# Output projection and gate as seven block products with 512 columns, weight sums formed by adding transfers

## Chip, cores and metric

One core of one Trainium2 chip. The metric is the device time of one execution in microseconds. TensorE multiplies, VectorE and ScalarE work element by element, GpSimd and SyncE (SP) have queues of their own, and 16 DMA engines move data for every queue.

## What is computed

One layer of a hybrid trunk on 1024 tokens of width 1024, in float32, and a final norm:

```python
u = rms_norm(h, norm_w)
proj = u @ w_in                       # 1024 x 6668, split into the mixers' inputs
o_hg = group_rms_norm(hgrn2_mixer(q, f_logit, i_in, lb), hg_norm_w, 6) * silu(g_hg)
o_pool = pool_mixer(u_pool, pool_w, pool_scale) * silu(g_pool)
y_ssd = ssd_mixer(xbc, dt_raw, ...) * silu(z)
o_ssd = group_rms_norm(y_ssd, ssd_norm_w, 4)
mixed = concatenate([o_hg, o_pool, o_ssd])       # 1024 x 2048
h = h + mixed @ w_out                            # output projection
gate = sigmoid(h @ w_pg)
h = h + gate * (p_i @ w_pe)                      # p_i: 1024 x 256
return rms_norm(h, final_norm_w)
```

## The kernel before

Every float32 product is made of three matmuls on rounded operands: a number is split into `hi` (a cast by ScalarE) and `lo` (the remainder, a subtraction by VectorE), and `mm3` (L163) issues hi x hi, hi x lo and lo x hi. Weights come by `wload` (L130, 512 KB on SP's queue, two buffers `raw`) and are split by `wsplit` (L135, four buffers). `bank` (L96) hands out eight PSUM banks by tags (`mx`, `pj`, `sc`).

The stages in order: the x norm with its transposes into `uh`/`ul` (the tokens transposed, hi and lo) and the v tiles; pool mixing and the gates of the hg part, both already by seven products of two by two blocks (`st_cm`, L327, and `st_tm`, L361, whose sums of weights VectorE makes in `st_cm_w`, L307, and `add`, L371); six hg heads; four SSD groups (L827); the g tiles (L894); the output projection (L927); the gate (L979) and the final norm.

The output projection runs over two halves of the 2048 mixed columns (`ab`) and four pieces of 256 output columns (`q`). For each it makes eight token tiles by `tm_tile` (L182): 8 blocks of 128 x 3 matmuls of 256 columns. `he` adds the bank into `H`, at first together with x (`xr`, 128 KB loads). The operands are put into `uh`/`ul` by `fill` (L846): 96 transposes, a ScalarE and a VectorE op for each bank of four. The y part is multiplied by silu(z) (`z_gate`, L880) and normalised (`y_norm`, L919) between the tiles of `q` = 1. `h_back` (L863) transposes `H` back into `uh`/`ul`. The gate takes four pieces of 256 columns x eight tiles x (24 + 6 for p @ w_pe), then sigmoid, product, sum, square, scaling (L990 to L1002), and in the last piece the root on GpSimd (L1005), the last scaling and the store of 512 KB.

A scheduler orders each engine's instructions by priorities: `high_priority` moves an instruction ahead, `issue_after` holds one back. Each engine and each queue then works in that order, so whatever waits holds all that stands behind it on the same engine.

## Time and profile before

| | us |
|---|---|
| median of 3 runs (1051.61 to 1053.7) | 1052.12 |
| the profiled execution | 1054.85 |
| its span in the trace | 1053.0 |
| TensorE busy in the span | 1027.2 |
| VectorE busy | 620.3 |
| ScalarE busy | 447.9 |
| GpSimd busy | 39.9 |

The span is the time from the first to the last recorded event of the profiled execution; 1.85 us lie around it. Matmuls overlap in the array, so that the sum of their durations is more than the time that they take; where TensorE is busy without a gap, the distance of two starts is the price of one.

### The profile page before, as it was taken

Reading aid. Unit: us, or ns where it says so; the run is one execution under the profiler, and the core shown is the slowest. Engines: PE = TensorE matmul, PEld = TensorE weight load, DVE = VectorE, ACT = ScalarE, POOL = GpSimd, SP = SyncE. Lnnn points to the kernel's source line nnn. Section 1 sums busy time; section 2 is a strip of 40 time slices with the busy share of each in tenths; the row PEclk is TensorE's granted clock in tenths of the full one; section 3 lists DMA queues with packets and bytes.
Section 4 is the critical chain, followed back from the end, with each engine's and each line's share of the span. In section 5 each row is a group of like instructions: output and inputs, shape, how many; then the busy total and the mean of one; then the engine's idle time right before and its main releaser. Section 6 shows DMA issues by size and latency. Waiting matters only on the chain.

```text
span 1053.0 us, 19902 instructions
## 1 busy us (share of the span) xinstructions
PE 1027.2 (98%) x8364; PEld 923.7 (88%) x8364; DVE 620.3 (59%) x1156; ACT 447.9 (43%) x904; POOL 39.9 (4%) x69
## 2 busy tenths in 40 slices
...
GB/s 293 128 66 63 40 100 119 83 61 200 163 22 41 41 22 21 52 41 21 59 72 57 85 40 81 121 139 96 93 118 87 50 141 41 41 41 41 2 21 141
DMA packets 41434, 82.73 MB, mean 79 GB/s; under 512 B 4000, under 2 KB 26880, under 8 KB 41088
## 3 DMA queue, kind: packets, MB, share of 16 engines
...
q14 instruction: 25, 0.20, 0.1%
...
## 4 chain that ended last, share of the span: by engine, by line
PE 81%; DVE 11%; ACT 3%; DMA 3%; issue 1%; POOL 0%; SPq 0%; POOLq 0%; ACTq 0%; DVEq 0%
PE b_pj L166 19%; PE b_pj L165 19%; PE b_pj L167 19%; DVE ar L582 5%; PE b_mx L165 3%; PE b_mx L167 3%; PE b_mx L166 3%; PE b_mx L806 1%; DVE lo L140 1%; PE b_sc L704 1%; PE b_mx L699 1%; PE b_mx L701 1%; DVE blk L601 1%; PE b_sc L167 1%; PE b_sc L166 1%; PE b_sc L165 1%
## 5 line engine op out<-in xcount | busy, mean ns | idle before, releaser
L165 PE MATMUL b_pj<-hi,uh 128*128 128x256 f32 (+1 forms) x1088 | 309.9, 285 | 0.4 <-ACT uh L216 0.4
L166 PE MATMUL b_pj<-lo,uh 128*128 128x256 f32 (+1 forms) x1088 | 307.3, 282 | 0.4 <-DVE lo L140 0.4
L167 PE MATMUL b_pj<-hi,ul 128*128 128x256 f32 (+1 forms) x1088 | 306.6, 282 | 0.2 <-DVE ul L217 0.2
L166 PEld LDWEIGHTS b_pj<-lo,uh 128*128 128x128 f32 x1088 | 205.8, 189 | 1.1 <-DVE lo L140 0.9
L165 PEld LDWEIGHTS b_pj<-hi,uh 128*128 128x128 f32 x1088 | 205.7, 189 | 0.8 <-ACT uh L216 0.6
L167 PEld LDWEIGHTS b_pj<-hi,ul 128*128 128x128 f32 x1088 | 205.5, 189 | 0.4 <-DVE ul L217 0.4
L166 PE MATMUL b_pj<-ul,hi 128*128 128x512 f32 x416 | 168.8, 406 | 0.0
L165 PE MATMUL b_pj<-uh,hi 128*128 128x512 f32 x416 | 168.3, 404 | 0.0
L167 PE MATMUL b_pj<-uh,lo 128*128 128x512 f32 x416 | 167.8, 403 | 0.0
L139 ACT CAST hi<-raw 128x1024 fp32r<-128x1024 f32 (+1 forms) x72 | 73.9, 1026 | 175.6 <-PE b_pj L167 99.0
L140 DVE TENSOR_TENSOR lo<-raw,hi 128x1024 fp32r<-128x1024 f32 (+1 forms) x72 | 85.9, 1194 | 103.5 <-ACT hi L139 91.7
L582 DVE TENSOR_TENSOR ar<-ar 128x512 f32<-128x512 f32 (+8 forms) x168 | 93.9, 594 | 6.5 <-PE b_sc L673 5.0
L166 PEld LDWEIGHTS b_pj<-ul,hi 128*128 128x128 f32 x416 | 78.2, 188 | 17.7
L165 PEld LDWEIGHTS b_pj<-uh,hi 128*128 128x128 f32 x416 | 78.2, 188 | 16.9
L167 PEld LDWEIGHTS b_pj<-uh,lo 128*128 128x128 f32 x416 | 78.2, 188 | 16.7
L748 DVE SCALAR_TENSOR_TENSOR ar<-ar,pr 128x1021 f32<-128x1021 f32 (+2 forms) x42 | 53.7, 1279 | 0.6
L954 DVE TENSOR_TENSOR big<-xr,b_pj 128x256 f32<-128x256 f32 x32 | 13.4, 419 | 50.6 <-PE b_pj L167 50.6
L782 ACT ACTIVATE E<-E,sm 128x128 f32<-128x128 f32 x96 | 32.0, 392 | 25.3 <-DMA E<-cumd 21.0
L956 DVE TENSOR_TENSOR big<-big,b_pj 128x256 f32<-128x256 f32 x32 | 13.4, 419 | 43.5 <-PE b_pj L167 43.5
L1001 ACT ACTIVATE junk<-sg 128x256 f32<-128x256 f32 x32 | 13.4, 418 | 40.2 <-DVE sg L999 40.2
L140 DVE TENSOR_TENSOR lo<-big,hi 128x1024 fp32r<-128x1024 f32 x18 | 21.9, 1222 | 14.0 <-ACT hi L139 14.0
L739 ACT COPY ar<-b_pj 128x512 f32<-128x512 f32 x28 | 16.2, 580 | 31.9 <-PE b_pj L167 31.8
...
## 6 DMA issues: line engine op xcount, KB each, us to landing
raw<-wcm SPq DMA_DIRECT2D x34, 512.0 KB, 3.2
raw<-wo SPq DMA_DIRECT2D x16, 512.0 KB, 3.8
raw<-wtm SPq DMA_DIRECT2D x12, 512.0 KB, 3.2
...
x<-x SPq DMA_DIRECT2D x8, 512.0 KB, 9.4
...
raw<-wg SPq DMA_DIRECT2D x8, 512.0 KB, 3.4
```

The lines of the kernel that those rows point to most:

```text
L139: A.copy(hi[:, :width], raw[:, :width])
L140: V.tensor_tensor(out=lo[:, :width], in0=raw[:, :width], in1=hi[:, :width].bitcast(F32), op=ALU.subtract)
L165: T.matmul(out=o, lhsT=sh, rhs=mh, start=first, stop=False, skip_group_check=more)
L166: T.matmul(out=o, lhsT=sh, rhs=ml, start=False, stop=False, skip_group_check=more)
L167: T.matmul(out=o, lhsT=sl, rhs=mh, start=False, stop=last, skip_group_check=more)
L582: mul = lambda o, x, y: V.tensor_tensor(out=o, in0=x, in1=y, op=ALU.mult)
L739: A.copy(xp[:, c], b)
L748: V.scalar_tensor_tensor(out=y[:, d:], in0=xp[:, : S - d], scalar=cw(i), in1=y[:, d:], op0=ALU.mult, op1=ALU.add)
L782: A.activation(E[:, i, :], E[:, i, :], AF.Relu, scale=-1.0, bias=cum[:, r0 + i : r0 + i + 1])
L954: V.tensor_tensor(out=H[:, t, qc], in0=xr, in1=b, op=ALU.add)
L956: V.tensor_tensor(out=H[:, t, qc], in0=H[:, t, qc], in1=b, op=ALU.add)
L1001: A.activation(junk, sg, AF.Square, accum_out=ssf[:, q, t : t + 1])
```

## The change

- **The products.** The output projection and the gate are each computed as seven products of two by two blocks (`Seven`). A block of tokens is 512 tokens, a block of columns 512 columns; the inner dimension is halved too, into 4 groups of 256 for the projection and 2 for the gate. All matmuls have 512 columns. A product adds into four banks, and banks are read into `H`, or into `Q` for the gate, with signs. Sums of tokens are made by VectorE (`tokens`), sums of weights lie ready in DRAM.
- **Sums of weights.** `sums_by_dma` forms the four sums that a set of weights needs by eight transfers from DRAM to DRAM, four of which add to what lies there. There are eight sets: four for `st_cm` (`tcd`, 256 KB each transfer), two for `st_tm` (`ttd`, 512 KB), one for the projection (`tod`, 2 MB), one for the gate (`tgd`, 1 MB). All 64 are issued by GpSimd's queue after the last root of the x norm. VectorE's sums in `st_cm_w` and `st_tm` are gone, some signs change.
- **Operands through DRAM.** `fill` still transposes; ScalarE copies the bank out and GpSimd's queue stores it (`mtd`). When the last tile is stored, 20 loads on GpSimd's queue bring the operands into `Q` (8 MB, in the space of `uh`/`ul` and others), and 8 more bring x into `H`. The products split tokens group by group (`asplit`). `h_back` puts `H` back into `Q` by ScalarE alone.
- **p @ w_pe** is computed apart, in 16 tiles of 512 columns: 8 ahead of the first product, 8 within the gate; ScalarE's queue stores them (`ped`) and SP loads them for the gate.
- **The y part** is multiplied and normalised by `y_fin` at the end of each SSD group.
- **The gate's end** works on tiles of 128 x 512 (`gate`, `close`); for the second 512 tokens an adding transfer puts the product into `H`.

The diff, without the renamed layouts of weights on the host:

```diff
+    PAIRS_C = ((26, 27), (30, 31), (28, 29), (32, 33))
+    PAIRS_T = ((5, 6), (7, 2))
+    tcd = [dp.tile([P, 2048], F32, name=f"tcd{i}") for i in range(4)]
+    ttd = [dp.tile([P, 4096], F32, name=f"ttd{i}") for i in range(2)]
+    tod = dp.tile([4, 4 * P, 1024], F32, name="tod")
+    tgd = dp.tile([4, 2 * P, 1024], F32, name="tgd")
+    def sums_by_dma(d, b11, b12, b21, b22):
+        t1, t3, t2, t4 = d
+        add = lambda o, i: nc.gpsimd.dma_start(out=o, in_=i, accum_op=ALU.add, max_dma_last_dim=8192)
+        nc.gpsimd.dma_start(out=t3, in_=b22)
+        nc.gpsimd.dma_start(out=t1, in_=b11)
+        add(t3, b12)
+        add(t1, b12)
+        nc.gpsimd.dma_start(out=t2, in_=t3)
+        add(t2, b11)
+        nc.gpsimd.dma_start(out=t4, in_=t2)
+        add(t4, b21)
...
+    with tc.issue_after(rooted.ins):
+        for d, (j0, j1) in zip(tcd, PAIRS_C):
+            sums_by_dma([d[:, i * 512 : i * 512 + 512] for i in range(4)], wcm[j0][:, :512], wcm[j1][:, :512], wcm[j0][:, 512:], wcm[j1][:, 512:])
+        for d, (s0, s1) in zip(ttd, PAIRS_T):
+            sums_by_dma([d[:, i * 1024 : i * 1024 + 1024] for i in range(4)], wtm[2 * s0], wtm[2 * s1], wtm[2 * s0 + 1], wtm[2 * s1 + 1])
+        sums_by_dma([tod[i] for i in range(4)], *(wo[i, j] for i in range(2) for j in range(2)))
...
-    def st_cm_w(j0, j1):
...
-            V.tensor_tensor(out=t1, in0=b12, in1=b11, op=ALU.subtract)
-            V.tensor_tensor(out=t3, in0=b22, in1=b12, op=ALU.subtract)
...
+    def st_cm_w(i):
+        j0, j1 = PAIRS_C[i]
+        w0 = wsplit(wload(wcm[j0], 1024), 1024)
+        w1 = wsplit(wload(tcd[i][:, :1024], 1024), 1024)
+        w2 = wsplit(wload(tcd[i][:, 1024:], 1024), 1024)
+        w3 = wsplit(wload(wcm[j1][:, 512:], 512), 512)
...
+    def st_tm(i, fin):
+        s0, s1 = PAIRS_T[i]
+        srcs = {1: wtm[2 * s0], 2: wtm[2 * s0 + 1], 3: wtm[2 * s1 + 1]}
+        for n, z in enumerate((5, 7, 6, 4)):
+            srcs[z] = ttd[i][:, n * 1024 : n * 1024 + 1024]
...
-        G.memset(a, 0.0)
+        V.memset(a, 0.0)
...
+    def y_fin(g, half):
+        ts, gs = slice(4 * half, 4 * half + 4), slice(g * DG, (g + 1) * DG)
+        sg, sgh = ar.take(768)
+        sg = sg.rearrange("p (c n) -> p c n", n=DG)
+        nc.sync.dma_start(sg, gzd[:, ts, gs])
+        V.tensor_tensor(out=Y[:, ts, gs], in0=Y[:, ts, gs], in1=sg, op=ALU.mult)
+        ar.give(sgh)
+        for t in range(4 * half, 4 * half + 4):
+            junk = sp.tile([P, 256], F32, tag="junk", bufs=1, name="junk")
+            A.activation(junk[:, :DG], Y[:, t, gs], AF.Square, accum_out=ssy[:, g, t : t + 1])
+        rstd(rsy[:, g, ts], ssy[:, g, ts], DG)
+        V.tensor_tensor(out=Y[:, ts, gs], in0=Y[:, ts, gs], in1=rsy[:, g, ts].unsqueeze(2).broadcast_to([P, 4, DG]), op=ALU.mult)
...
+        for half in range(2):
+            y_fin(g, half)
...
+    def fill(src, wcol, ab, half, k):
+        b = bank("mx")
+        for i in range(4):
+            T.transpose(out=b[:, i * P : (i + 1) * P], in_=src[:, half * 4 + i, k * P : (k + 1) * P], identity=ident)
+        z, zh = ar.take(512)
+        with tc.high_priority(offset=EPRIO):
+            A.activation(z, b, AF.Copy, scale=pr[:, wcol + k : wcol + k + 1])
+        nc.gpsimd.dma_start(mtd[half][ab][:, k, :], z)
...
-            for t in range(NT):
-                tm_tile("o", q, 256, t, he, pcs)
-                if q == 0 and t < 3:
-                    fill_step(*((O, P_HW, 0), (Y, P_SW, 2))[ab], 1, t)
-                if ab == 0 and q == 3 and 4 <= t < 7:
-                    fill_step(Y, P_SW, 2, 0, t - 4)
-                if ab == 0 and q == 1:
-                    z_gate(t)
-                    y_norm(t)
...
+    def pe_tile(sg, aw, ew, half, j, t, engine):
+        (ah, al), (eh, el) = aw, ew
+        b = bank("pj")
+        for k in range(2):
+            c, w = slice(k * 512 + t * P, k * 512 + t * P + P), slice(k * 512, k * 512 + 512)
+            mm3(b, ah[:, c], al[:, c], eh[:, w], el[:, w], k == 0, k == 1)
+        with tc.high_priority(offset=EPRIO):
+            engine(sg, b)
+        nc.scalar.dma_start(ped[:, 4 * half + t, HALF[j]], sg)
...
+    for j in range(2):
+        for t in range(4):
+            pe_tile(xw[t][:, :512], pw[0], pw[1 + j], 1, j, t, V.tensor_copy)
...
+    Q = [[fp.tile([P, KD, 512], F32, name=f"q{i}{j}") for j in range(2)] for i in range(2)]
+    for i in range(2):
+        for j in range(2):
+            for g in range(3):
+                nc.gpsimd.dma_start(Q[i][j][:, 2 * g : 2 * g + 2, :], mtd[i][j][:, 2 * g : 2 * g + 2, :])
+            for k in range(2):
+                last = nc.gpsimd.dma_start(Q[i][j][:, 6 + k, :], pod[2 * j + k][:, HALF[i]])
+    with tc.issue_after(last.ins):
+        for t in range(NT):
+            nc.gpsimd.dma_start(H[:, t, :], x[t * P : (t + 1) * P, :])
...
+    def asplit(src):
+        hi = fp.tile([P, 2, 512], F32R, tag="ah", bufs=4, name="ah")
+        lo = fp.tile([P, 2, 512], F32R, tag="al", bufs=4, name="al")
+        with tc.high_priority(offset=WPRIO):
+            A.copy(hi, src)
+            V.tensor_tensor(out=lo, in0=src, in1=hi.bitcast(F32), op=ALU.subtract)
+        return hi, lo
...
+    class Seven:
+        def __init__(self, q, n, w, td):
+            self.q, self.n, self.w = q, n, {1: w[0, 0], 2: w[1, 0], 3: w[1, 1], 5: td[0], 7: td[1], 6: td[2], 4: td[3]}
+        def tokens(self, i, g):
+            a11, a12, a21, a22 = (self.q(r, c, g) for r in range(2) for c in range(2))
+            s2 = S2[:, g]
+            with tc.high_priority(offset=WPRIO):
+                if i == 6:
+                    V.tensor_tensor(out=a21, in0=a11, in1=a21, op=ALU.subtract)
+                    V.scalar_tensor_tensor(out=s2, in0=a22, scalar=-1.0, in1=a21, op0=ALU.mult, op1=ALU.subtract)
+                elif i == 5:
+                    V.scalar_tensor_tensor(out=a11, in0=s2, scalar=-1.0, in1=a11, op0=ALU.mult, op1=ALU.subtract)
+                elif i == 3:
+                    V.scalar_tensor_tensor(out=a12, in0=s2, scalar=-1.0, in1=a12, op0=ALU.mult, op1=ALU.subtract)
+            return asplit({1: a11, 2: a12, 3: a12, 4: a22, 5: a11, 6: s2, 7: a21}[i])
+        def load(self, i, g):
+            return wload(self.w[i][g * P : (g + 1) * P, :], 1024)
+        def mult(self, bs, i, first, evac, by_tile=False):
+            gs = []
+            for g in range(self.n):
+                raw = self.load(i, g)
+                gs.append((self.tokens(i, g), wsplit(raw, 1024)))
+                if not by_tile:
+                    self.part(bs, gs, g, range(4), first)
+            for t in range(4):
+                if by_tile:
+                    for g in range(self.n):
+                        self.part(bs, gs, g, (t,), first)
+                evac(t, bs[t])
+        def part(self, bs, gs, g, ts, first):
+            (ah, al), (bh, bl) = gs[g]
+            for k in range(2):
+                w = slice(k * 512, k * 512 + 512)
+                for t in ts:
+                    c = slice(t * P, (t + 1) * P)
+                    mm3(bs[t], ah[:, k, c], al[:, k, c], bh[:, w], bl[:, w], first and g == 0 and k == 0, g == self.n - 1 and k == 1, not first)
...
+    def onto(i, j, op):
+        def f(t, b):
+            h = H[:, 4 * i + t, HALF[j]]
+            with tc.high_priority(offset=EPRIO):
+                V.tensor_tensor(out=h, in0=h, in1=b, op=op)
+        return f
+    sev = Seven(lambda r, c, g: Q[r][c][:, 2 * g : 2 * g + 2, :], 4, wo, tod)
+    X = four("mx", "mx", "mx", "mx")
+    sev.mult(X, 1, True, onto(0, 0, ALU.add))
+    sev.mult(four("pj", "pj", "sc", "sc"), 2, True, onto(0, 0, ALU.add))
+    sev.mult(X, 6, False, onto(0, 1, ALU.subtract))
+    sev.mult(X, 7, False, onto(1, 1, ALU.subtract))
+    sev.mult(X, 4, False, onto(1, 0, ALU.add))
+    Yb = four("pj", "pj", "sc", "sc")
+    sev.mult(Yb, 5, True, onto(1, 1, ALU.subtract))
+    for t in range(4, 8):
+        h_back(t, 0, "mx")
+    for t in range(4):
+        h_back(t, 0, "mx")
+    for t in range(4, 8):
+        h_back(t, 1, "mx")
+    sev.mult(Yb, 3, False, onto(0, 1, ALU.subtract))
...
+    def gate(i, j, t, src):
+        sg, tt = gq(i, j, t), 4 * i + t
+        h = H[:, tt, HALF[j]]
+        r = rsf[:, tt : tt + 1]
+        pe = fp.tile([P, 512], F32, tag="pe", bufs=3, name="pe")
+        nc.sync.dma_start(pe, ped[:, tt, HALF[j]])
+        with tc.high_priority(offset=EPRIO):
+            A.activation(sg, src, AF.Sigmoid)
+        with tc.high_priority(offset=300):
+            V.tensor_tensor(out=sg, in0=sg, in1=pe, op=ALU.mult)
+            if i == 0:
+                V.tensor_tensor(out=h, in0=h, in1=sg, op=ALU.add)
+            else:
+                nc.gpsimd.dma_start(out=h, in_=sg, accum_op=ALU.add)
+            A.activation(sg, h, AF.Square, accum_out=ssf[:, j, tt : tt + 1])
+            if j == 0:
+                V.tensor_scalar(out=r, in0=ssf[:, 0, tt : tt + 1], scalar1=1.0 / D, scalar2=EPS, op0=ALU.mult, op1=ALU.add)
+                V.tensor_tensor(out=h, in0=h, in1=fwb[:, HALF[0]], op=ALU.mult)
+            else:
+                G.tensor_scalar(out=r, in0=ssf[:, 1, tt : tt + 1], scalar1=1.0 / D, scalar2=r, op0=ALU.mult, op1=ALU.add)
+                G.tensor_tensor(out=r, in0=r, in1=negh[:, :1], op=ALU.pow)
+                V.scalar_tensor_tensor(out=h, in0=h, scalar=r, in1=fwb[:, HALF[1]], op0=ALU.mult, op1=ALU.mult)
+                h0 = H[:, tt, HALF[0]]
+                A.activation(h0, h0, AF.Copy, scale=r)
+        if j == 1:
+            nc.sync.dma_start(out[tt * P : (tt + 1) * P, :], H[:, tt, :])
...
+    sev = Seven(lambda r, c, g: Q[r][0][:, 4 * c + 2 * g : 4 * c + 2 * g + 2, :], 2, wg, tgd)
+    X = four("mx", "mx", "mx", "mx")
+    pw = [pe_part(pT, 0), pe_part(we, 0)]
+    sev.mult(X, 1, True, keep(0, 0, 1.0))
+    for t in range(4):
+        pe_tile(fp.tile([P, 512], F32, tag="pst", bufs=4, name="pst"), *pw, 0, 0, t, A.copy)
+    pw[1] = pe_part(we, 1)
+    sev.mult(X, 6, False, keep(0, 1, -1.0))
+    for t in range(4):
+        h_back(t, 1, "sc")
+    for t in range(4):
+        pe_tile(fp.tile([P, 512], F32, tag="pst", bufs=4, name="pst"), *pw, 0, 1, t, A.copy)
+    sev.mult(X, 7, False, keep(1, 1, -1.0))
+    sev.mult(X, 4, False, lambda t, b: gate(1, 0, t, b))
+    Yb = four("pj", "pj", "sc", "sc")
+    sev.mult(Yb, 5, True, close(1, 1, ALU.subtract))
+    sev.mult(four("mx", "mx", "mx", "mx"), 2, True, close(0, 0, ALU.add), True)
+    sev.mult(Yb, 3, False, close(0, 1, ALU.subtract), True)
```

Three places in the order of instructions. First SP's queue where the weights of the first `st_cm` are loaded, between stores of v tiles (`vd`); before:

```order
L132 DMA raw<-wcm 128x1024
L229 DMA vd<-vs 128x256
L132 DMA raw<-wcm 128x1024
L229 DMA vd<-vs 128x256 x9
L132 DMA raw<-wcm 128x1024
L229 DMA vd<-vs 128x256 x6
L132 DMA raw<-wcm 128x1024
```

and after (`tcd_97` is the first set of sums, 256 KB x 8):

```order
L155 DMA raw<-wcm 128x1024
L253 DMA vd<-vs 128x256
L155 DMA raw<-tcd_97 128x1024
L253 DMA vd<-vs 128x256 x8
L155 DMA raw<-tcd_97 128x1024
L155 DMA raw<-wcm 128x512
L253 DMA vd<-vs 128x256 x7
```

In the place of the second load of raw weights stands a load of the first half of the sums, and in that of the third one of their second half; behind each stand stores of v tiles.

Second ScalarE's queue between the last fill and the first product of the output projection; before (L219 is a fill, L139 the cast of a weight, L216 that of a pool part):

```order
L219 ACTIVATE uh<-b_mx,pr 128x512 x2
L922 ACTIVATE junk,ssy<-ar 128x192
L139 CAST hi<-raw 128x1024
L216 CAST uh<-ar 128x512
L900 ACTIVATE sg<-b_pj 128x256
L216 CAST uh<-ar 128x512
L139 CAST hi<-raw 128x1024
L219 ACTIVATE uh<-b_mx,pr 128x512 x6
L139 CAST hi<-raw 128x1024 x6
L216 CAST uh<-ar 128x512 x2
```

and after (L868 is a fill, L162 the cast of a weight, L926 the store of a p @ w_pe tile, L959 the cast of tokens):

```order
L162 CAST hi<-raw 128x1024
L868 ACTIVATE ar<-b_mx,pr 128x512 x3
L926 DMA ped<-big 128x512 x2
L926 DMA ped<-xw_4848 128x512
L162 CAST hi<-raw 128x1024
L926 DMA ped<-xw_4849 128x512
L926 DMA ped<-big 128x512 x2
L926 DMA ped<-xw_4848 128x512
L162 CAST hi<-raw 128x1024 x2
L926 DMA ped<-xw_4849 128x512
L959 CAST ah<-q_7598 128x1024 x4
```

The fills are followed by eight stores, each of which waits for VectorE's copy of its tile, and the casts of the first tokens stand behind the last of them.

Third VectorE at the end of the gate; before, where each tile has its reads, sums and scalings in a row:

```order
L1002 TENSOR_TENSOR big<-sg,fwb 128x256
L1008 TENSOR_SCALAR big<-big,rsf 128x576
L998 TENSOR_TENSOR sg<-sg,b_sc 128x256
L999 TENSOR_TENSOR sg<-big,sg 128x256
L1002 TENSOR_TENSOR big<-sg,fwb 128x256
L1008 TENSOR_SCALAR big<-big,rsf 128x576
L998 TENSOR_TENSOR sg<-sg,b_mx 128x256
L999 TENSOR_TENSOR sg<-big,sg 128x256
L1002 TENSOR_TENSOR big<-sg,fwb 128x256
L1008 TENSOR_SCALAR big<-big,rsf 128x576
```

and after, from the last read of a bank of product 2 on (L1077 reads a bank, L1049 multiplies by p @ w_pe, L1051 adds to h, L1057 and L1061 scale):

```order
L1077 TENSOR_TENSOR q_7599<-q_7599,b_mx 128x512
L1061 SCALAR_TENSOR_TENSOR big<-big,rsf,fwb 128x512 x2
L1051 TENSOR_TENSOR big<-big,q_7599 128x512
L1077 TENSOR_TENSOR q_7599<-q_7599,b_pj 128x512
L1061 SCALAR_TENSOR_TENSOR big<-big,rsf,fwb 128x512 x2
L1049 TENSOR_TENSOR q_7599<-q_7599,pe 128x512
L1077 TENSOR_TENSOR q_7599<-q_7599,b_pj 128x512
L1056 TENSOR_SCALAR rsf<-ssf 128x1
L1057 TENSOR_TENSOR big<-big,fwb 128x512
L1051 TENSOR_TENSOR big<-big,q_7599 128x512
L1049 TENSOR_TENSOR q_7599<-q_7599,pe 128x512 x2
L1077 TENSOR_TENSOR q_7599<-q_7599,b_sc 128x512
```

Sixteen more rows of these kinds follow there. Reads of product 3's banks stand between the rows of tiles of the products before it.

## Rows read from the trace of the kernel before

**Rows 1.** The page: span, then busy us and share of each engine.

```profile
span 1053.0 us, 19902 instructions
...
PE 1027.2 (98%) x8364; PEld 923.7 (88%) x8364; DVE 620.3 (59%) x1156; ACT 447.9 (43%) x904; POOL 39.9 (4%) x69
```

**Rows 2.** Stretches of 50 us: busy us (count) by engine, granted clock, DMA share, GB/s.

```profile
50.00:100.00 50.00, 49.33 (x366) 46.92 (x366) 33.29 (x48) 18.94 (x30) 0.00 (x0) 1.00 0.19 65
...
500.00:550.00 50.00, 48.90 (x314) 39.73 (x313) 36.56 (x73) 27.77 (x56) 0.00 (x0) 1.00 0.22 69
...
750.00:800.00 50.00, 50.00 (x425) 50.00 (x424) 11.71 (x21) 4.20 (x4) 0.00 (x0) 1.00 0.28 90
```

**Rows 3.** Timeline of TensorE, 512 columns: start us, duration us, line, operation.

```profile
111.73 0.39 PE L165 MATMUL b_mx<-uh,hi 128*128 128x512 f32 x1
...
113.82 0.40 PE L165 MATMUL b_pj<-sh,hi 128*128 128x512 f32 x1
```

**Rows 4.** Shorter stretches, columns as in rows 2.

```profile
180.00:184.20 4.20, 2.54 (x19) 2.14 (x18) 1.23 (x1) 1.04 (x1) 0.00 (x0) 0.99 0.78 258
184.20:187.40 3.20, 2.88 (x14) 2.59 (x13) 0.00 (x0) 1.20 (x4) 0.00 (x0) 0.50 0.04 15
...
727.00:730.20 3.20, 0.95 (x9) 0.71 (x8) 3.20 (x10) 3.06 (x10) 0.00 (x0) 1.00 0.11 34
730.20:733.60 3.40, 3.40 (x17) 3.40 (x18) 2.59 (x8) 3.27 (x13) 1.20 (x2) 0.50 0.02 8
```

**Rows 5.** Groups by shape, VectorE, then ScalarE: busy us, mean ns, idle before.

```profile
L140 DVE TENSOR_TENSOR lo<-raw,hi 128x1024 fp32r<-128x1024 f32 x66 | 80.6, 1222 | 103.4 <-ACT hi L139 91.7 <-PE b_mx L167 4.5 <-PE b_pj L167 4.5
...
L883 DVE TENSOR_TENSOR ar<-ar 128x768 f32<-128x768 f32 x8 | 7.6, 950 | 1.1 <-DMA ar<-gzd 1.1
...
L320 DVE TENSOR_TENSOR big<-raw,big 128x512 f32<-128x512 f32 x4 | 2.8, 688 | 0.1
...
L139 ACT CAST hi<-raw 128x1024 fp32r<-128x1024 f32 x66 | 69.2, 1048 | 168.5 <-PE b_pj L167 98.0 <-PE b_pj L166 61.9 <-PE b_sc L166 4.0
...
L739 ACT COPY ar<-b_pj 128x512 f32<-128x512 f32 x28 | 16.2, 580 | 31.9 <-PE b_pj L167 31.8
...
L922 ACT ACTIVATE junk<-ar 128x192 f32<-128x192 f32 x32 | 11.6, 364 | 5.5 <-DVE ar L883 4.8
```

**Rows 6.** Timeline of TensorE, 16 transposes and the next matmul.

```profile
930.07 1.92 PE L868 MATMUL b_mx<-ident,big 128*128 128x128 f32 x16
931.74 0.36 PE L165 MATMUL b_pj<-hi,uh 128*128 128x256 f32 x1
```

**Rows 7.** Timelines at the end: the last matmul, then the last ScalarE operation.

```profile
1045.45 0.28 PE L167 MATMUL b_mx<-eh,pl 128*128 128x256 f32 x1
...
1048.35 0.67 ACT L1007 ACTIVATE big<-big,rsf 128x448 f32<-128x448 f32 x1 [1.03 <-POOL rsf L1006]
```

**Rows 8.** The page, DMA issues: count, KB each, median us from issue to landing.

```profile
raw<-wcm SPq DMA_DIRECT2D x34, 512.0 KB, 3.2
...
x<-x SPq DMA_DIRECT2D x8, 512.0 KB, 9.4
```

**Rows 9.** Timeline of SP's queue: start us, time from first to last issue, line.

```profile
47.52 0.33 SPq L132 DMA_DIRECT2D raw<-wcm  x1
...
71.14 0.38 SPq L132 DMA_DIRECT2D raw<-wcm  x1
```

**Rows 10.** Timeline of GpSimd: start us, duration us, line, operation.

```profile
30.51 0.55 POOL L127 TENSOR_TENSOR rsx<-rsx,negh 128x1 f32<-128x1 f32 x1
...
315.14 0.20 POOL L126 TENSOR_SCALAR rsh<-ssh 128x8 f32<-128x8 f32 x1 [105.03 <-ACT junk L716]
...
493.82 2.67 POOL L127 TENSOR_TENSOR rsh<-rsh,negh 128x8 f32<-128x8 f32 x1
```

**Rows 11.** Stretches at the start, columns as in rows 2.

```profile
0.00:26.00 26.00, 21.73 (x139) 19.03 (x140) 15.91 (x21) 16.23 (x29) 6.12 (x19) 1.00 0.79 296
10.00:15.00 5.00, 3.65 (x25) 3.01 (x26) 4.04 (x6) 4.00 (x8) 2.37 (x4) 1.00 1.02 414
```

284 lines of the change are left out of this document (90 added, 194 removed).

## Prediction

> **What bounds the kernel now.** I read the share of busy time first, then the span in stretches of 50 us, then the starts of single matmuls. TensorE is busy 98% of the span, VectorE 59%, ScalarE 43% [rows 1]. The stretches show that this is no mean over unlike stages: from 750 to 800 us, inside the output projection, TensorE is busy 50.00 of 50.00 us with VectorE at 11.71 [rows 2]. Nothing is waited for there, so that stage lasts as long as its matmuls. The listed duration of a matmul is no price, since neighbours overlap; the price is the distance of two starts. With 256 columns, 425 matmuls in 50.00 us give 0.1176 us each [rows 2]. With 512 columns nine steps lie between 111.73 and 113.82 us, 0.232 us each [rows 3]. Twice the columns cost 1.97 times as much: width alone gains next to nothing, and what counts is how many columns are streamed in all.
>
> **The products.** The output projection before has 2 halves x 4 column pieces x 8 token tiles x 24 = 1536 matmuls, the gate 4 x 8 x (24 + 6) = 960, all of 256 columns: 2496 x 0.1176 = 293.5 us. After, the projection has 7 products x 4 groups x 24 = 672, the gate 7 x 2 x 24 = 336, the p @ w_pe tiles 16 x 6 = 96, all of 512: 1104 x 0.232 = 256.1 us. **Minus 37.4 us**, all on the path, as TensorE never waits there. The 96 + 64 transposes stay.
>
> **What goes besides.** (a) The sums of weights leave VectorE. Where the first gate product starts (180 to 187.4 us) TensorE idles 1.66 + 0.32 us and then runs 3.2 us at a granted clock of 0.50 (1.2 of 2.4 GHz), which loses 1.6 [rows 4]. Its operands waited behind loads and sums; with finished sums one load and one split are left. I take all of it, **minus 3.6** (bounds 0 and 3.6). (b) Normalising y and filling the operands no longer sit among projection tiles. There TensorE idles 2.25 us at 727 us and then runs 3.4 us at 0.50, losing 1.7 [rows 4]: **minus 4.0** (bounds 0 and 4.0). (c) That normalisation moves into the four SSD groups: per group 4 products of 768 elements at 0.95 us on VectorE, 3.8 us, and 8 squares of 0.36 on ScalarE, 2.9 us [rows 5]. VectorE is busy 36.56 of 50 us there [rows 2], so it would reach about 40; ops behind each other on an engine with a fifth to spare need not reach TensorE. In turn 24 VectorE splits of the fills go. I take **0** (bounds -3 and +3).
>
> **What comes.** (d) The start of the first product. ScalarE's queue holds the stores of the p @ w_pe tiles, each waiting for VectorE's copy of that tile, ahead of the cast of the first tokens. So after the last of these tiles stand, with TensorE idle: the copy of 512 from PSUM (0.69, taken from the 512-wide sum), the store's issue (0.33, as SP's), the cast (1.05) and the remainder (1.22) [rows 5, 9]: 3.3 us. The idle stretch at 727 us, shorter than this, was followed by 3.4 us at half clock [rows 4]; I add its 1.7. **Plus 5** (bounds 3 and 8). The loads of the tokens run meanwhile behind eight tiles x 6 x 0.232 = 11.1 us. (e) Twelve banks of four transposes each come in a row between two products: 16 transposes before take 1.67 us to the next matmul's start, 0.104 each [rows 6], so 48 take 5.0 us, while ScalarE copies the banks out at 0.58 each [rows 5], 7.0 us; the first copies overlap the product: **plus 1.5** (0 to 3). (f) At some ten product boundaries a bank must be read before the next product adds to it; a read of 0.69 can find VectorE inside an op of 1.22. Before shows no such wait. **Plus 1.5** (0 to 6).
>
> (g) The end. Before, the last matmul starts at 1045.45 us and the span ends at 1053.0 [rows 1], 7.3 us after its end; the last ScalarE op ends at 1049.02 and the store takes the other 4.0 us [rows 7]. After, VectorE has, behind the last matmul of the gate's product 5: 12 reads of banks, 12 products with p @ w_pe, 8 sums into h, 5 + 8 scalings by the final weight, all of 512 elements, 45 x 0.69 = 31.1 us, and three splits, 3.7 us; with the small ops 35.3 and the gaps 37 us. TensorE has two products of 48 x 0.232, 22.3 us. VectorE becomes the engine that ends last. With about 1 us of waiting for the last square and root and the 4.0 us of the last store, the span ends some 42 us after product 5, 20 us after the last matmul. **Plus 12**. Bounds: plus 7 if the waits vanish and part of it fits earlier, plus 18 if the sums into h by accumulating transfers, for which squares and VectorE's rows wait, take 9.4 us instead of some 4 (no accumulating transfer is in the trace; the loads of 512 KB land after 3.2 us alone and 9.4 us with eight queued [rows 8]).
>
> **The sum.** -37.4 - 3.6 - 4.0 + 0 + 5 + 1.5 + 1.5 + 12 = **-25.0 us**. The rows come from an execution of 1054.85 us with a span of 1053.0, of which the sum makes 1028.0. Timed runs have a median of 1052.12, 2.73 below the profiled execution, and the sum taken from it gives **1027 us**. With the bounds of these terms, not all at one end at once, this case's own range is 1013 to 1036.
>
> **Rival 1, the sums of weights come too late (slower at its far end).** The 64 transfers from memory to memory wait for one another in GpSimd's queue from 31.1 us on, after the last root [rows 10]. The first st_cm needs the set tcd0: its first half two dependent steps on, its second half six. Before, SP asked for weights at 47.52 and 71.14 us [rows 9]. If SP waits there, v stores stand behind it; with four staging buffers and a tile of 24 x 0.1176 = 2.8 us, TensorE goes on for about 9 us. So a step may last (71.1 + 9 - 31.1) / 6 = 8.2 us free of charge, and each us more costs 6. At 9.4 us, the price of a queued load, it costs 7 us (1034). At 12.4 us per step the whole gain of 25 us is gone, and **above that the kernel is slower than before**. For it: no transfer between memory and memory, none that adds, and none from GpSimd's queue is in the trace; each adds 256 KB to 2 MB to 40 MB in all. Against it: a 512 KB load needs 3.2 us [rows 8], twice the bytes of such a step, and between 50 and 100 us the transfer engines are busy 0.19 of the time [rows 2]. GpSimd's next own work is at 315.14 us [rows 10]; until then 40 MB need 141 GB/s, where 414 was moved at the start [rows 11]. The pace of issue is a second way to the same end: no row has GpSimd issue a transfer, SP takes 0.33 us for one [rows 9], and the longest of GpSimd's roots took 2.67 us [rows 10]. At 2.67 us per issue tcd0's last add, the 21st transfer in the queue, goes out at 31.1 + 20 x 2.67 = 84.5 us and lands near 88, 8 us too late: **1035 us**. VectorE's ops of that stretch are two-input ones at 1.2 ns per element [rows 5], the form that ran beside GpSimd's roots of 0.55 us as well, so I give this way 0.05 and the slow steps 0.12, of which 0.08 beyond 12.4 us. The page "SBUF — State Buffer" of the Trainium skill says ("Who interferes with whom") that GpSimd cannot write a transfer's descriptors while VectorE runs an op in a two-port mode, which two-input ops lack, and gives ("A bandwidth-pool intuition that's wrong") 3.1 us in place of 0.62 for a transfer beside such an op. By it, as an estimate, the 21st would go out at 93 us and the time be 1044 if VectorE ran such ops throughout; no run here shows GpSimd issuing beside them.
>
> **Rival 2, tokens and x starve the second product.** 8 MB of tokens, then 4 MB of x, come by 28 loads in GpSimd's queue. In VectorE's order the split for the last group of product 2 stands behind the sums for product 6 and the first sum into h, so 8.5 MB must be there within 39 us of the products' start, 49 us of the first request: 173 GB/s beside 94 GB/s of weights (512 KB per 5.57 us). The first 26 us of the kernel moved 296 GB/s, and at best 414 [rows 11]; that speaks against it. If GpSimd's queue brings 130 GB/s, 8.5 MB take 65 us and TensorE waits 16 us less some catching up: plus 14, **1041 us**. Chance 0.13.
>
> **Rival 3, the SSD groups cannot hold the added work.** If VectorE's 3.8 us per group lie on its chain of products and sums between TensorE's steps and two thirds show, plus 10: **1037 us**. For it: VectorE at 36.56 of 50 us has little to spare in an SSD group's bursts. Against it: TensorE is busy 48.90 of 50 in the same stretch [rows 2]. Chance 0.10.
>
> **How the numbers follow.** Forecast 0.60, rivals 0.17, 0.13 and 0.10. A measurement of this kernel can tell about 0.2%, 2 us, from no change. Slower than 1054.2: the far part of rival 1, 0.08, and 0.04 for two mishaps at once, 0.12. Within 2 us: 0.04. Faster: 0.84. The range must leave out no more than 2 in 10: below 1013 I see 0.05, and with the near part of rival 1 and rivals 2 and 3 inside, it runs to **1045**; the far part of rival 1 stays out.
>
> **What would show it.** Right: 512-wide matmuls 0.232 us apart and some 257 us of them in the products; no idle at the first gate product; an idle of about 3 us and then half clock ahead of product 1; VectorE busy without a gap for some 20 us behind the last matmul. Rival 1 shows as SP waiting for GpSimd's transfers before 90 us and TensorE idle between v tiles; rival 2 as a token split or a sum into h that a transfer releases, with TensorE idle inside product 2; rival 3 as TensorE waits on VectorE between 500 and 700 us. The forecast is wrong at its root if TensorE is not busy throughout the seven products, that is, if VectorE's splits and sums (two splits and up to two sums per 5.57 us) pace them.

## Result and profile after

The changed kernel is **slower**: 1102.41 us median (1097.85 to 1105.98) against 1051.86 for the kernel before beside it, a ratio of 1.047 with a 95% interval of 1.043 to 1.052. The forecast was 1027 us in a range of 1013 to 1045; both the sign and the size were wrong.

The page of the profiled execution after (1105.98 us), its lines on the span, the busy time, the clock, the transfers and their queues:

```profile
span 1104.1 us, 17389 instructions
...
PE 1002.3 (91%) x6972; PEld 846.3 (77%) x6972; DVE 659.0 (60%) x1073; ACT 495.8 (45%) x924; POOL 119.7 (11%) x191
...
PEclk9999987869899999999999999999989999999995
DMA  7899999997472101101012221333499322224555
...
q1 hardware_dynamic: 47344, 96.08, 26.0%
q0 software_dynamic: 14464, 62.92, 21.9%
```

TensorE is busy 25 us less than in [rows 1] and yet has 102 us without work. The row of the transfer engines says where to look: from the second slice to the ninth, some 30 to 250 us, they are full, and in that stretch the granted clock of TensorE sinks. Around 800 to 850 us they are full again, and the last slice has the clock at half. The queue of software transfers, which did not exist before, takes 21.9% of 16 engines for 63 MB.

Three points of time divide the loss. GpSimd's roots of the six hg heads are markers that stand in both traces. Before, the first starts at 315.14 us [rows 10], and the sixth, from GpSimd's timeline of before (start us, duration us, line, operation, idle before):

```profile
493.35 0.38 POOL L126 TENSOR_SCALAR rsh<-ssh 128x8 f32<-128x8 f32 x1 [37.41 <-ACT junk L716]
```

The first and the sixth after:

```profile
376.17 0.20 POOL L149 TENSOR_SCALAR rsh<-ssh 128x8 f32<-128x8 f32 x1 [115.79 <-ACT junk L710]
...
555.09 0.42 POOL L149 TENSOR_SCALAR rsh<-ssh 128x8 f32<-128x8 f32 x1 [38.36 <-ACT junk L710]
```

And TensorE's last matmul after, to set against the first row of [rows 7]:

```profile
1075.39 0.40 PE L190 MATMUL b_sc<-hi,al 128*128 128x512 f32 x1
```

| stretch | before, us | after, us | difference | forecast |
|---|---|---|---|---|
| start to the first root | 315.1 | 376.2 | +61.0 | -3.6 |
| first to sixth root | 178.2 | 178.9 | +0.7 | 0 |
| sixth root to the end of the last matmul | 552.4 | 520.7 | -31.7 | -33.4 |
| end of the last matmul to the end | 7.3 | 28.3 | +21.0 | +12 |
| span | 1053.0 | 1104.1 | +51.1 | -25 |

The third line is the gain that the change was forecast to bring, nearly to the microsecond. It is more than lost ahead of the hg heads, where the change puts no matmul and takes none away (2167 up to the first root in both traces), and again at the end.

Stretches after (columns as in [rows 2]); the second belongs beside the first line of [rows 2], the last three are the fills ahead of the products, the stretch in which these start, and one inside them:

```profile
31.00:50.00 19.00, 16.34 (x140) 16.14 (x138) 14.01 (x11) 7.15 (x12) 8.06 (x13) 1.00 0.95 243
50.00:100.00 50.00, 49.20 (x365) 47.55 (x365) 31.07 (x39) 17.82 (x27) 15.14 (x22) 0.97 1.01 215
100.00:150.00 50.00, 42.55 (x177) 32.29 (x177) 20.24 (x28) 16.89 (x25) 10.58 (x16) 0.97 1.01 274
150.00:200.00 50.00, 35.43 (x122) 25.75 (x123) 19.55 (x29) 11.74 (x17) 5.19 (x8) 0.80 0.99 264
200.00:250.00 50.00, 32.36 (x189) 30.36 (x188) 13.42 (x13) 12.25 (x21) 3.90 (x6) 0.76 1.03 281
...
750.00:800.00 50.00, 49.96 (x454) 48.85 (x451) 28.21 (x79) 33.31 (x71) 15.35 (x25) 1.00 0.44 155
800.00:850.00 50.00, 41.91 (x174) 32.57 (x173) 33.68 (x36) 17.98 (x20) 16.60 (x31) 0.93 0.97 375
850.00:900.00 50.00, 50.00 (x218) 40.64 (x217) 38.66 (x38) 18.09 (x18) 0.00 (x0) 1.00 0.38 141
```

The transfer engines have a share of 1.0 for 200 us, and again from 800 to 850 us. From 31 to 50 us TensorE idles 2.7 us (before: none), between 50 and 100 us only 0.8 us; from 100 to 250 us it idles 39.7 us of 150 and runs at 0.76 to 0.97 of its clock besides.

What it waits for is in the chain that ended last, rows from 133 to 254 us (start us, duration us, what; a transfer's duration runs from its issue to its landing):

```profile
133.59 18.20 DMA raw<-wcm
151.81 0.63 ACT hi L162
152.46 0.70 DVE lo L163
153.18 15.12 DMA raw<-tcd
...
170.72 11.27 DMA raw<-wcm
...
202.34 11.49 DMA raw<-ttd
...
216.24 22.69 DMA raw<-ttd
...
241.28 12.64 DMA raw<-wtm
```

Load, cast, remainder, load: the chain is SP's loads of weights one after the other, at 11 to 23 us each. It holds loads of sums (`tcd`, `ttd`), but also of raw weights (`wcm`, `wtm`), which depend on no sum at all. The view of the transfers after, issues on SP's queue and the first sums on GpSimd's (count, KB each, median us from issue to landing):

```profile
raw<-tod SPq DMA_DIRECT2D x16, 512.0 KB, 3.2
...
tcd<-wcm POOLq DMA_DIRECT2D x24, 256.0 KB, 7.9
...
raw<-tcd SPq DMA_DIRECT2D x8, 512.0 KB, 8.0
raw<-ttd SPq DMA_DIRECT2D x8, 512.0 KB, 11.5
```

A load of 512 KB of sums costs 8.0 and 11.5 us while GpSimd's transfers run, and 3.2 us for `tod`, long after them: the figure of [rows 8]. So the picture to be tried: the 64 transfers keep the 16 engines full from 31 us to about 260 us, and every load of the kernel in that time lands late.

### The profile page after: what moved, and what is told of

It reads as the page before. It is cut to its first block, busy times and chain, and to the rows that moved or that the text cites. A ratio compares the mean times of both kernels' runs of the same rounds, so it can differ in the third digit from the quotient of the medians.

```text
span 1104.1 us, 17389 instructions
## 1 busy us (share of the span) xinstructions
PE 1002.3 (91%) x6972; PEld 846.3 (77%) x6972; DVE 659.0 (60%) x1073; ACT 495.8 (45%) x924; POOL 119.7 (11%) x191
## 3 DMA queue, kind: packets, MB, share of 16 engines
q0 software_dynamic: 14464, 62.92, 21.9%
HBM read 136.97 MB, written 66.11 MB: 184 GB/s over the span
## 4 chain that ended last, share of the span: by engine, by line
PE 61%; DMA 13%; DVE 12%; ACT 5%; issue 3%; POOL 1%; POOLq 0%; ACTq 0%; DVEq 0%
PE b_pj L188 10%; PE b_pj L189 10%; PE b_pj L190 10%; PE b_mx L188 6%; PE b_mx L189 6%; PE b_mx L190 6%; DVE ar L576 4%; DMA raw<-ttd 3%; DMA raw<-wcm 3%; ACT hi L162 2%; DVE lo L163 2%; PE b_sc L188 2%; PE b_sc L189 2%; PE b_sc L190 1%; DMA gzd<-sg 1%
## 5 line engine op out<-in xcount | busy, mean ns | idle before, releaser
L163 DVE TENSOR_TENSOR lo<-raw,hi 128x1024 fp32r<-128x1024 f32 (+1 forms) x114 | 137.0, 1204 | 177.0 <-ACT hi L162 176.1
L162 ACT CAST hi<-raw 128x1024 fp32r<-128x1024 f32 (+1 forms) x114 | 117.6, 1034 | 168.0 <-PE b_pj L189 52.5
L188 PE MATMUL b_pj<-hi,uh 128*128 128x256 f32 (+1 forms) x320 | 93.1, 291 | 3.5 <-ACT vs L252 3.2
L189 PE MATMUL b_pj<-lo,uh 128*128 128x256 f32 (+1 forms) x320 | 91.9, 287 | 0.2 <-DVE lo L163 0.2
L190 PE MATMUL b_pj<-hi,ul 128*128 128x256 f32 (+1 forms) x320 | 91.6, 286 | 0.2 <-DVE ul L241 0.2
L188 PE MATMUL b_mx<-hi,ah 128*128 128x512 f32 x208 | 83.0, 399 | 4.8 <-ACT ah L959 4.8
L190 PE MATMUL b_mx<-hi,al 128*128 128x512 f32 x208 | 82.4, 396 | 0.4 <-DVE al L960 0.4
L189 PE MATMUL b_mx<-lo,ah 128*128 128x512 f32 x208 | 82.7, 397 | 0.0
L959 ACT CAST ah<-q 128x1024 fp32r<-128x1024 f32 x36 | 37.4, 1046 | 93.1 <-PE b_mx L189 71.7
L188 PEld LDWEIGHTS b_pj<-hi,uh 128*128 128x128 f32 x320 | 61.2, 191 | 4.1 <-ACT vs L252 3.4
L189 PEld LDWEIGHTS b_pj<-lo,uh 128*128 128x128 f32 x320 | 61.2, 191 | 0.9 <-DVE lo L163 0.7
L190 PEld LDWEIGHTS b_pj<-hi,ul 128*128 128x128 f32 x320 | 61.2, 191 | 0.5 <-DVE ul L241 0.4
```

What stands on the lines that cost most here:

```text
L162: A.copy(hi[:, :width], raw[:, :width])
L163: V.tensor_tensor(out=lo[:, :width], in0=raw[:, :width], in1=hi[:, :width].bitcast(F32), op=ALU.subtract)
L188: T.matmul(out=o, lhsT=sh, rhs=mh, start=first, stop=False, skip_group_check=more)
L189: T.matmul(out=o, lhsT=sh, rhs=ml, start=False, stop=False, skip_group_check=more)
L190: T.matmul(out=o, lhsT=sl, rhs=mh, start=False, stop=last, skip_group_check=more)
L959: A.copy(hi, src)
```

## Experiments

S is the theory that the sums cost by **occupying the transfer engines**; D that they cost by **dependence**: a load must wait until its sum has been made. Sizes named as 8, 16, 24 or 40 MB are in units of 1024 x 1024 bytes; 40 of them are 41.94 MB as the profile counts. All ratios are to the kernel before, with 95% intervals.

**The two big sets later.** The sums for the projection and the gate (24 of the 40 MB) are issued after the first root of the hg heads; the sums that `st_cm` and `st_tm` wait for stay where they are.

```diff
-        sums_by_dma([tod[i] for i in range(4)], *(wo[i, j] for i in range(2) for j in range(2)))
-        sums_by_dma([tgd[i] for i in range(4)], *(wg[i, j] for i in range(2) for j in range(2)))
...
-        rstd(rsh[:, h, :], ssh[:, h, :], P)
+        r = rstd(rsh[:, h, :], ssh[:, h, :], P)
+        if h == 0:
+            with tc.issue_after(r.ins):
+                sums_by_dma([tod[i] for i in range(4)], *(wo[i, j] for i in range(2) for j in range(2)))
+                sums_by_dma([tgd[i] for i in range(4)], *(wg[i, j] for i in range(2) for j in range(2)))
```

> The changed kernel, only that the 16 transfers for the sums of w_out and w_pg (tod, tgd, 24 MB) are issued after the first hg head's root (some 315 to 376 us) and not at the start. Theory S (the transfer engines are full: in the changed kernel their share is 1.0 from 50 to 250 us, and every load of that stretch lands late): 48 small transfers of 16 MB remain there, the stretch of full share ends before 150 us, and TensorE's idle of some 50 us between 100 and 300 us shrinks to 15 or less: 1055 to 1065 us. Theory D (the loads wait for the sums they read, whatever the engines' share): the sets of st_cm are as late as before, those of st_tm somewhat earlier: 1080 to 1095.

Measured: 1048.9 us, 0.9955 (0.9939 to 0.9971). Below what S named and far below D. Two lines of this kernel, the stretch of the hg heads in which the big sums now run (columns as in [rows 2]):

```profile
315.00:450.00 135.00, 130.39 (x1526) 105.63 (x1526) 96.95 (x217) 47.91 (x126) 20.59 (x24) 1.00 0.82 219
```

and its first root:

```profile
320.08 0.20 POOL L149 TENSOR_SCALAR rsh<-ssh 128x8 f32<-128x8 f32 x1 [166.70 <-ACT junk L708]
```

24 MB moved away bring 53.5 us of the kernel's time and 56.1 us at the first root. Among the heads they cost nothing: a share of 0.82 over 135 us, a clock of 1.00, and 178.8 us from the first root to the sixth (320.08 to 498.86), against 178.2 before. The heads load little (a share of 0.10 over the same time in the kernel before), and nothing there shows a wait for the transfer engines.

**No sums at all.** No transfer of sums is issued; raw weights of the same size are loaded in their place, so that what comes out are other products.

```diff
-    with tc.issue_after(rooted.ins):
-        for d, (j0, j1) in zip(tcd, PAIRS_C):
...
-        w1 = wsplit(wload(tcd[i][:, :1024], 1024), 1024)
+        w1 = wsplit(wload(wcm[j0], 1024), 1024)
...
-            srcs[z] = ttd[i][:, n * 1024 : n * 1024 + 1024]
+            srcs[z] = wtm[2 * (s0, s1)[n // 2] + n % 2]
```

> The changed kernel without the 64 adding and copying transfers; in place of a sum the loads read raw weights of the same size, so that all products work on other numbers and the output is another. Both theories: the first hg head's root comes at about 312 us instead of 376, nothing else moves, and the time is 1104 less 61 to 64, so 1040 to 1044 us. Were it 1028, the forecast of all other steps had been right; above 1050 the sums were not the main cause.

Measured: 1039.82 us, 0.9879 (0.9864 to 0.9894), just below what was expected. This kernel's stretch that holds the first gate product, its software queue on the page, and its first root:

```profile
150.00:200.00 50.00, 50.00 (x316) 43.65 (x315) 28.46 (x37) 22.04 (x36) 0.00 (x0) 1.00 0.40 127
```

```profile
q0 software_dynamic: 6592, 20.98, 5.8%
```

```profile
309.71 0.20 POOL L149 TENSOR_SCALAR rsh<-ssh 128x8 f32<-128x8 f32 x1 [278.60 <-ACT junk L703]
```

All sums together cost the kernel 62.6 us (1102.41 - 1039.82). The first root comes 5.4 us earlier than before: what the forecast hoped for from taking the sums off VectorE exists. Its size is known only roughly, since this mark moves between kernels with the same early part: in the five below in which VectorE makes these sums it stands at 313.02 to 315.84 us, 3.3 to 6.1 us later than here, where 3.6 us were named.

**Sums made, not read.** All 64 transfers are issued as in the changed kernel, but the loads read raw weights as above; only the products of the projection and the gate still read their sums. Nothing in `st_cm` and `st_tm` depends on a sum.

```diff
-        w1 = wsplit(wload(tcd[i][:, :1024], 1024), 1024)
+        w1 = wsplit(wload(wcm[j0], 1024), 1024)
...
-            srcs[z] = ttd[i][:, n * 1024 : n * 1024 + 1024]
+            srcs[z] = wtm[2 * (s0, s1)[n // 2] + n % 2]
```

> The changed kernel with all 64 transfers for the sums, but st_cm and st_tm load raw weights of the same size instead of the sums, so that none of their loads waits for a sum (the output is another). Theory S: the share of the transfer engines stays 1.0 and the loads stay late, 1085 to 1100 us. Theory D: no load waits any more, 1042 to 1050.

Measured: 1098.49 us in a single run, as S had it. Of the 62.6 us, 58.7 stay where no load waits for a sum. The stretch of this kernel that lies in `st_tm`:

```profile
200.00:250.00 50.00, 30.68 (x201) 29.40 (x200) 9.97 (x10) 10.21 (x19) 3.55 (x5) 0.76 1.02 286
```

Share 1.02, TensorE at 30.68 of 50 us, the clock at 0.76: the same picture as in the changed kernel. S holds. What is left for D is 3.9 us, and the changed kernel's own four runs spread over 8.1 us: D is small at most, and not told from nothing.

**Copies in place of adding transfers.** The same 64 transfers of the same sizes, none of which adds.

```diff
-        add = lambda o, i: nc.gpsimd.dma_start(out=o, in_=i, accum_op=ALU.add, max_dma_last_dim=8192)
+        add = lambda o, i: nc.gpsimd.dma_start(out=o, in_=i, max_dma_last_dim=8192)
```

> The changed kernel with the 32 adding transfers for the sums made plain copies of the same sizes (the sums are then not formed, the output is another). If adding costs the transfer engines extra time: the stretch of full share is shorter by a third or more, and the time falls to 1060 to 1080. If an added byte costs what a copied one does: within 5 us of the changed kernel.

Measured: 1078.89 us in a single run, a span of 1077.1; the time lies in the band for a price of adding, while the stretch of full share ends near 200 us in place of 255, a quarter shorter and not a third. The software queue of this kernel:

```profile
q0 software_dynamic: 13440, 62.92, 17.3%
```

This prices a transfer by engine time. After: 21.9% of 1104.1 us is 241.8 us of all 16 engines; without sums 5.8% of 1037.5, 60.2; with copies 17.3% of 1077.1, 186.3. So 41.94 MB of sums take 181.6 us, and as copies 126.1 us, 3.0 us per MB (333 GB/s). Half of the 64 add; with the other half at the copies' price, 63.1 us, the adding half takes 118.5 us for 20.97 MB: **5.65 us per MB, 177 GB/s, 1.88 times a copy**. These are averages over transfers of 256 KB to 2 MB. Adding is what makes over a third of the loss (23.5 of 62.6 us), and the rest is there with copies alone. Whether the engines themselves or the memory at both ends of these transfers set this pace was not tried. The page "Collectives: The Full Stack" of the Trainium skill says ("The bandwidth ceiling: the fold count and why AG ≠ RS ≠ AR") that an adding transfer must read two sources where a copy reads one, and gives a ratio of 1.93 between two collectives; the 1.88 here, between DRAM and DRAM on one core, is near it, but the second read itself does not show: the profile counts 136.97 MB read with the adding transfers and with the copies alike.

**VectorE makes the small sums again.** As the first experiment, and `st_cm_w` and `st_tm` add on VectorE as before; no transfer of sums runs ahead of the heads.

```diff
+        with tc.high_priority(offset=WPRIO):
+            V.tensor_tensor(out=t1, in0=b11, in1=b12, op=ALU.add)
+            V.tensor_tensor(out=t3, in0=b22, in1=b12, op=ALU.add)
+        w1 = wsplit(T_[:, :1024], 1024)
...
```

> e1_late_big, with the sums for st_cm and st_tm made by VectorE again as in the kernel before (with the new signs) in place of 48 transfers. In e1 the first hg root comes at 320.1 us, without any sums at 309.7, in the kernel before at 315.1. If the 16 MB of small transfers cost what is left there, the root comes at 314 to 316 and the time is 1043 to 1045 us. If VectorE's sums cost no less than the transfers do, the time stays at 1049.

Measured: 1041.82 us, 0.9905 (0.9879 to 0.9931), below the band expected. Its first root and its last matmul:

```profile
313.02 0.20 POOL L149 TENSOR_SCALAR rsh<-ssh 128x8 f32<-128x8 f32 x1 [281.70 <-ACT junk L738]
```

```profile
1011.58 0.39 PE L190 MATMUL b_sc<-hi,al 128*128 128x512 f32 x1
```

The 16 MB of small sums by transfer thus cost 7.1 us on the way to that root against VectorE's own sums (320.08 there). In this pair of traces VectorE's own sums cost 3.3 us against none (309.71); over all kernels here with either early part it is 4 to 10 us (320.08 to 322.63 in three, 313.02 to 315.84 in five) and 3 to 6 us.

**GpSimd adds into h at the end.** As the first experiment; in `gate` GpSimd adds in place of VectorE and of the adding transfers.

```diff
-            if i == 0:
-                V.tensor_tensor(out=h, in0=h, in1=sg, op=ALU.add)
-            else:
-                nc.gpsimd.dma_start(out=h, in_=sg, accum_op=ALU.add)
+            G.tensor_tensor(out=h, in0=h, in1=sg, op=ALU.add)
```

> e1_late_big, with the sums into h in the gate made by a GpSimd op for all 16 tiles, in place of 8 accumulating transfers and 8 VectorE ops. If the wait for the accumulating transfers (VectorE idle 3.9 us at 1070.9 in the changed kernel, issue to landing 6.9 us) and VectorE's load lengthen the end, the 28 us from the last matmul to the end become 16 to 22, and the time 1037 to 1043 us. If the end is a chain of waits that no single op makes, or if GpSimd's op takes over 2 us, 1047 to 1052.

Measured: 1048.49 us, 0.9958 (0.9941 to 0.9975), no gain over the first experiment. GpSimd's add of 512 takes 1.6 us on average, where VectorE's takes 0.69, and VectorE's products with p @ w_pe take 0.87 us in this kernel in place of 0.69. From the last matmul's end to the end of the span it is 29.2 us, against 27.8 in the first experiment.

**Other buffers for the p @ w_pe tiles.** As the first experiment; the eight tiles ahead of product 1 have six staging buffers in place of four, and SP stores them in place of ScalarE.

```diff
-        nc.scalar.dma_start(ped[:, 4 * half + t, HALF[j]], sg)
+        q.dma_start(ped[:, 4 * half + t, HALF[j]], sg)
...
+    pst = [big[:, 6144 + i * 512 : 6656 + i * 512] for i in range(4)] + [xw[2][:, :512], xw[3][:, :512]]
-            pe_tile(xw[t][:, :512], pw[0], pw[1 + j], 1, j, t, V.tensor_copy)
+            pe_tile(pst[(4 * j + t) % 6], pw[0], pw[1 + j], 1, j, t, V.tensor_copy, nc.sync)
```

> e1_late_big, with six buffers in place of four for the eight p @ w_pe tiles ahead of the first product, and their stores on SP's queue in place of ScalarE's. If TensorE's idle of 8 us ahead of product 1 (and the 3.4 us at half clock behind it) comes from copies that wait for the stores of the tiles four before, which land late beside the loads of the tokens, 3 to 6 us go: 1043 to 1046 us. If the tokens themselves come no earlier, it stays within 1.5 us of 1049.

Measured: 1050.61 us, 0.9984 (0.9969 to 1.0000); no gain. TensorE's first matmul of product 1 in this kernel, and ScalarE's cast ahead of the tokens, from the two timelines:

```profile
764.94 0.80 PE L188 MATMUL b_mx<-hi,ah 128*128 128x512 f32 x1 [8.00 <-ACT ah L962]
```

```profile
762.89 1.04 ACT L162 CAST hi<-raw 128x1024 fp32r<-128x1024 f32 x1 [5.11 <-DMA raw<-wo]
```

The waits among the tiles are nearly gone (0.21 us), and 8.0 us of idle stand in one piece: the cast of the tokens stands behind that of a weight whose load lands late. The buffers were not what the transition waits for.

**Three in one.** VectorE's small sums, GpSimd's adds and the six buffers together; against the VectorE sums alone:

```diff
-        nc.scalar.dma_start(ped[:, 4 * half + t, HALF[j]], sg)
+        q.dma_start(ped[:, 4 * half + t, HALF[j]], sg)
...
-                V.tensor_tensor(out=h, in0=h, in1=sg, op=ALU.add)
-            else:
-                nc.gpsimd.dma_start(out=h, in_=sg, accum_op=ALU.add)
+            G.tensor_tensor(out=h, in0=h, in1=sg, op=ALU.add)
```

> e5, e6 and e7 in one kernel. If the three gains lie in different stretches they add up: 1028 to 1034 us, 2% under the kernel before.

Measured: 1044.16 us, 0.9918 (0.9903 to 0.9933): missed, and not better than the VectorE sums alone. Its VectorE and GpSimd timelines, where the adds run side by side with VectorE's remainders:

```profile
977.80 1.22 DVE L163 TENSOR_TENSOR lo<-raw,hi 128x1024 fp32r<-128x1024 f32 x1
...
985.23 2.31 DVE L163 TENSOR_TENSOR lo<-raw,hi 128x1024 fp32r<-128x1024 f32 x1
```

```profile
980.89 5.56 POOL L1083 TENSOR_TENSOR big<-big,q 128x512 f32<-128x512 f32 x3 [193.83 <-DVE q L1082]
```

The op of 1.22 us takes 2.31 while GpSimd adds. The page "SBUF — State Buffer" of the Trainium skill says ("Who interferes with whom") that a VectorE op with two inputs in SBUF contends with a GpSimd op that reads SBUF; the trace agrees. The work handed to GpSimd here slows the engine that it was to relieve.

**A gate without blocks.** VectorE's small sums, and the gate as four plain products of 512 x 512 with 96 matmuls each, 384 in place of 336, the last of them tile by tile; no sums of the gate's weights, and VectorE adds into h.

```diff
...
-    sev.mult(X, 4, False, lambda t, b: gate(1, 0, t, b))
-    Yb = four("pj", "pj", "sc", "sc")
-    sev.mult(Yb, 5, True, close(1, 1, ALU.subtract))
-    sev.mult(four("mx", "mx", "mx", "mx"), 2, True, close(0, 0, ALU.add), True)
-    sev.mult(Yb, 3, False, close(0, 1, ALU.subtract), True)
+    plain(1, 1, t1, four("mx", "mx", "mx", "mx"))
+    plain(0, 0, t0, four("pj", "pj", "sc", "sc"))
+    plain(0, 1, t0, four("mx", "mx", "mx", "mx"), True)
```

> e5_dve_sums with the gate as plain products of 512 columns (384 matmuls in place of 336, four sets of four tiles, the last set tile by tile, no sums of w_pg, sums into h by VectorE). TensorE gets 48 x 0.232 = 11.1 us more. If the 26.5 us from the last matmul to the end in e5 come from four products that all release their tiles at the end, the end falls to 9 to 12 us, and the time to 1035 to 1039 us. If the end is as long as the work per tile makes it, whatever the order, it grows to 1050 or more.

Measured: **1034.25 us, 0.9827 (0.9811 to 0.9843)**: faster than both kernels, and below the band. The last matmul of this kernel, whose page gives a span of 1031.9:

```profile
1023.11 0.40 PE L190 MATMUL b_mx<-hi,al 128*128 128x512 f32 x1
```

From the last matmul's end to the end of the span 8.4 us remain, against 26.5 us with the gate in blocks and VectorE's small sums (last matmul's end, 1011.58 + 0.39, of 1038.5). 48 more matmuls, 11 us, buy 18 us of end. The edit changes two things at the end, though: the order in which products finish, and the eight adding transfers into h, which VectorE's adds replace. Blocks with VectorE's adds were not run. GpSimd's adds in the place of these transfers left the end at 29.2 us, but slowed VectorE besides; so the order is the likelier cause, and the share of each is not shown.

**Token loads staged.** VectorE's small sums; the loads of tokens and x are held back group by group behind the products' matmuls. It was also run with the plain gate.

```diff
+    q_load(0, 0)
+
+    def later(g, ins):
+        with tc.issue_after(ins):
+            if g < 3:
+                q_load((0, 1, 1)[g], (1, 0, 1)[g])
+            else:
+                for t in range(NT):
+                    nc.gpsimd.dma_start(H[:, t, :], x[t * P : (t + 1) * P, :])
```

> e5_dve_sums with the loads of the tokens and of x spread over the first product: only the first quarter (2 MB) at once, the next ones after the first matmul of each group. If TensorE's idle of 8 us ahead of product 1 and the half clock behind it come from loads and stores that share the transfer engines (share 1.0 there, weights and the stores of p @ w_pe land late) the idle falls to 3 to 4 us and the time to 1036 to 1039 us. If it is the chain of copy, store, cast and remainder alone, it stays at 1040 to 1043.

> e9 and e10 in one kernel. If both gains come as expected, 1029 to 1034 us.

Measured: 1058.95 us, 1.0064 (1.0047 to 1.0080), and with the plain gate 1048.3 us, 0.9961 (0.9947 to 0.9975). Both missed what every theory said. GpSimd's timeline of the first of the two:

```profile
760.75 1.08 POOL L985 DMA_DIRECT2D big<-x  x2 [12.76 <-DMA ped<-big]
761.84 1.60 POOL L973 DMA_DIRECT2D q<-mt  x3
```

and TensorE's waits for it, the largest of 700 to 860 us:

```profile
PE b_mx L188 <- ACT ah L999: 19.6, 1, 19.6
```

The edit did something else than meant: the scheduler put the loads of x ahead of the tokens in GpSimd's queue, where two of them stand 12.76 us for a buffer, and the first tokens go out only then. This says nothing on whether 12 MB at once disturb the start of product 1. It shows that the start hangs on the first tokens: 19.6 us of idle in place of the 4.75 ahead of that matmul with VectorE's sums alone.

## Why the prediction was wrong, point by point

**Rival 1 was the right place and the wrong price.** It named slow transfers of sums and gave 0.17 to them (0.05 of it to the pace of issue), 0.08 beyond the point at which the kernel gets slower. The forecast itself has no term for them, and they cost 62.6 us. The step that failed is how they were judged: by the time of one dependent step, free up to 8.2 us, and by bytes against the best rate seen, 40 MB at 141 GB/s where 414 had been moved [rows 11]. By its own measure it even passed: a step of `tcd` took 7.9 us (median), TensorE lost only 0.8 us from 50 to 100 us, and the sign that the prediction named, SP waiting for sums before 90 us, cost next to nothing. What counts was another thing. First, the engines' time per MB: sums move at 231 GB/s with all engines full (41.94 MB in 181.6 us), not 414. Second, the kernel's own traffic: without sums the share from 50 to 250 us is 0.26 to 0.52 (0.40 in the line above), so that the 229 us from 31 to 260 us hold some 135 us of free engine time by a mean share of 0.41, where 181.6 were wanted. Third, and the larger part: a stream that fills the engines delays whoever else loads, even where it would fit. The copies, 126.1 us, would just have fitted into the whole stretch, and still cost some 39 us (1078.89 - 1039.82, with a single run of the copies). The page "DMA: Bandwidth & Descriptors" of the Trainium skill says ("Issuing engines are not separate DMA queues") that transfers of all issuing engines end up on the same 16 engines and interleave there; the loads on SP's queue at 8.0 and 11.5 us beside GpSimd's stream, and 3.2 after it, agree. The reading "busy 0.19 between 50 and 100 us" [rows 2] was an argument for room, but it covers one stretch only, and the room of the whole stage has to be held against the transfers' engine time, for which no row stood in the trace before.

**The two paces of issue** that rival 1 added did not come. GpSimd's timeline after, the start of its stream (start us, duration us, line, operation, idle before):

```profile
31.14 0.78 POOL L128 DMA_DIRECT2D tcd<-wcm  x1
...
32.97 0.54 POOL L129 DMA_DIRECT2D tcd<-wcm  x1
36.06 2.62 POOL L127 DMA_DIRECT2D tcd<-wcm  x3 [2.55 <-DMA tcd<-wcm]
42.45 0.82 POOL L127 DMA_DIRECT2D tcd<-wcm  x1 [3.77 <-issue]
```

An issue takes 0.54 to 0.87 us, not 2.67 and not 3.1. The page "SBUF — State Buffer" of the Trainium skill ("A bandwidth-pool intuition that's wrong") has its 3.1 us beside a VectorE copy; VectorE ran mostly two-input ops here, and the trace shows no such delay.

**The end, term (g), was mis-sized:** +21.0 us in place of +12, beyond its upper bound of 18. Behind product 5 stood VectorE's ops as counted, but they began 3.5 us after its last matmul (end at 1053.55 us) and took 32.4 us of work from 1057.1 to 1100.15 us, in place of 37, with 10.7 us of waits where 1 us was allowed. VectorE's longest wait after, and the ScalarE square that it comes from:

```profile
1074.81 0.78 DVE L1061 SCALAR_TENSOR_TENSOR big<-big,rsf,fwb 128x512 f32<-128x512 f32 x1 [3.92 <-POOL rsf L1060]
```

```profile
1072.64 0.63 ACT L1054 ACTIVATE q<-big 128x512 f32<-128x512 f32 x1 [4.74 <-DMA big<-q]
```

An adding transfer into h holds a square, the square a root, the root VectorE. The prediction had this as its upper bound and set it at 18 by the price of a queued load. This wait is 3.9 of the 10.7 us; the others stand behind loads of p @ w_pe and the squares and roots of the last tiles. The plain gate shows what the end costs in all: with blocks, 12 of the 16 tiles come out in the last three products, 11 us apart, and with one product of 22 us for each four tiles, 8.4 us remain in place of 26.5 (with the adding transfers gone as well, as said above).

**The start of the first product, term (d), was mis-sized:** about +10 in place of +5, beyond its bound of 8. TensorE's timeline after, ahead of product 1:

```profile
811.26 0.50 PE L188 MATMUL b_pj<-hi 128*128 128x512 f32 x1 [1.49 <-DVE big L925]
...
814.33 0.50 PE L188 MATMUL b_pj<-hi 128*128 128x512 f32 x1 [1.40 <-DVE big L925]
...
820.75 0.80 PE L188 MATMUL b_mx<-hi,ah 128*128 128x512 f32 x1 [4.77 <-ACT ah L959]
...
822.40 0.80 PE L190 MATMUL b_mx<-hi,al 128*128 128x512 f32 x1 [0.43 <-DVE al L960]
```

That is 8.1 us of idle, and 0.50 of the clock for 5 us behind it, where nine matmuls stand 0.43 us apart in place of 0.23, which adds 1.7. The order was as foreseen (idle, then half clock, on the casts of the first tokens), but each step of it waits for a transfer while 12 MB of tokens and x are loaded; the share from 800 to 850 us is 0.97. That these loads are the cause is argued from the share and from the load of weights that the six buffers brought to light; the experiment that was to show it went wrong, so it stays open.

**What held.** The products: 218 matmuls in 50.00 us, 0.229 each, TensorE without a gap from 850 us on. (a): without early sums the first gate product has no idle (150 to 200 us, 50.00 of 50 at a clock of 1.00 in the kernel without sums). (b): 49.96 of 50 at 1.00 from 750 to 800 us after. (c): the SSD groups carry y's norm without loss. The last sum into their state, before and after:

```profile
699.04 0.35 DVE L820 TENSOR_TENSOR hst<-hst,b_sc 128x192 f32<-128x192 f32 x1
```

```profile
761.08 0.35 DVE L814 TENSOR_TENSOR hst<-hst,b_sc 128x192 f32<-128x192 f32 x1
```

That is 205.7 us behind the sixth root before and 206.0 after. (e) and (f) lie together with the products and came out some 3 us better than summed: from the sixth root to the last matmul -31.7, of which (d) makes +4.8 more than forecast. Rival 2 did not come, since product 2 has no idle; nor rival 3. With the sums costing nothing and (d) and (g) as they measured, the forecast's sum would have been 1053.0 - 25.0 + 4.8 + 9.0 = 1041.8 us of span; the kernel without sums has 1037.5.
